# Two transformer blocks on one core: all low parts of the mixers' weights on VectorE, softmax scaling, score copies and conv biases on ScalarE, conv steps at 1.3 per tile

## The chip, the core and the metric

The kernel runs on one core of a Trainium2 chip. The metric is the device time in microseconds (us) of one execution. The kernel before takes 2652.18 us, the median of three runs (2651.34 to 2655.23). One more execution was profiled; it took 2647.99 us, and its span, from the first to the last recorded instruction, is 2646.2 us.

## What is computed

The input is a sequence of 256 tokens of width 1024 in fp32, with a second sequence of 256 tokens, the context. A first block of two layers (called layer 0 and layer 1 here) runs over both sequences, then a second block of two layers runs over the first sequence alone. Only the first block's mixer matters for the change:

```python
proj = h @ p['w_in']                      # h: layernorm, scaled and shifted; 9760 columns
k, v, kg, vg, gf, gb = _mem_parts(...)    # attention keys/values; GLA keys/values, two log gates
q, qg, r, glu, gates = _rest_parts(...)
o_att = softmax(q k^T / sqrt(128)) v      # 8 heads of 128, 2 key/value heads
lg = log_sigmoid(glr @ w_a2 + b_a) / 16   # log gates, cumulated over the tokens
o_gla = gated linear attention, forwards and backwards, with exp(b_i - b_j) between tokens
y = a * sigmoid(g)                        # conv: depthwise, 31 taps, plus bias, layernorm, silu
out = (g_att * (o_att @ w_att_o) + g_gla * (o_gla' @ w_gla_o) + g_conv * (y' @ w_conv_o)) @ w_out
```

Layer 0 does this for both sequences, 512 tokens. Layer 1 does it for the first sequence, 256 tokens, and takes from the context only keys, values and gates. A feed-forward part of 2816 columns follows each mixer.

## The kernel before

**Products in two parts.** Every large product of fp32 operands is made of three TensorE products. An operand is split in a high part (a cast, `whi` for weights) and a low part (the operand minus its high part, `wlo`), and `mm_fm` (lines 386 to 388) and `mm_tm` (467 to 469) add high by high, high by low and low by high. The weights come from HBM as `raw` tiles of 1 MB; `wsplit` (line 357) makes the high part on ScalarE (line 362) and the low part by a subtraction (the helper `tt`, line 288). Which engine subtracts is decided by `pool_lo`: with 0 always VectorE, with 1 always GpSimd (the profile's POOL), with 2 every second time GpSimd:

```python
on_pool = self.pool_lo and self.nsplit % self.pool_lo == 0
```

There are three buffers each for high and low parts and two for `raw`. In the mixers `pool_lo` comes from `PLO0` and `PLO1`: the first number holds from the start of the mixer to the end of the attention's merge, the second from there on. `post`, which follows the mixer, sets it to 1 for its own products; the change leaves that as it is.

**A mixer's order of work.** After an opening in layer 0 that loads and normalizes the input, `mixer` projects the conv's two inputs a and g (16 tiles of 128 columns, 512 tokens wide in layer 0 and 256 in layer 1), then attention keys and values, queries, the gates' small input, and GLA keys and queries. Merge 0 projects the attention's output gates, flushes the attention and projects its result with `w_att_o`; merge 2 does the conv's output, merge 1 that of GLA.

**Background lanes.** Beside these projections run generators, called lanes: the conv's taps, the head transposes, attention, the gates, GLA scores and the modulation vectors (ada). After each tile (or each pair of weight rows) `tick` gives each lane its rate of steps, and `flush` runs a lane to its end. A step of `conv` is two taps for each of two channel groups, so four instructions (the helper `stt`, line 291); a pair of groups has 15 steps, and there are four pairs. `CRATE0 = 1.6` is the number of such steps per tile in layer 0, `CRATE1 = 1.0` in layer 1. Before merge 2 the lanes `gla` (gates) and `conv` are flushed, and `conv_norm` follows.

**What orders an engine's queue.** Instructions are traced in the order of this code, each with a priority. A scheduler then fixes one order for each engine from priorities and its own idea of when inputs are ready. Weight splits have a priority ahead of their place (`WP = -100`), taps one far behind (`CP = 600`). On the chip every engine executes its order as it stands, and an instruction that waits holds what is behind it.

**Names in the rows.** `ca` is a conv accumulator, `gt` the gated conv input, `cw` the taps' weights, `P` the softmax numerators, `PT` their transposes, `s` small columns such as maxima and reciprocals, `zm` and `e` the two terms of a log gate, `B` its cumulative sum, `eq` and `ek` the gate factors of GLA queries and keys, `A` GLA scores, `qn` and `ra` normalized and rotated heads, `pm` and `ps` PSUM tiles, `hTh` and `hTl` transposed heads.

Of the kernel before, what the change touches and what calls it, by code (L numbers as in the profile page):

```python
# [24 lines left out]
CRATE0 = 1.6  # L25
# [6 lines left out]
PLO0A = 1  # L32
PLO0B = 0
PLO0 = PLO0A, PLO0B
PLO1A = 2
# [152 lines left out]
class Builder:  # L188
# [383 lines left out]
    def tabs0(self):  # L572
        nc, I = self.nc, self.I
        rw = lambda n: I[n].rearrange("l (j p) -> (l j) p", p=128)
        self.vt0 = self.vectab("vt0", [rw("conv_b_dw"), rw("conv_ln_g"), rw("conv_ln_b"),
                                       I["gla_b_a"].rearrange("l d (j p) -> (l d j) p", p=128), rw("gla_norm")])
        self.vt0h = self.cp.tile([128, 68], F32, name="vt0h")
        self.ts(self.vt0h, self.vt0, 0.5)
        self.masks = self.cp.tile([128, 160], U32, name="masks")
        nc.sync.dma_start(self.masks, I["masks"])  # L580
        self.ptot = self.cp.tile([128, 2, 4], F32, name="ptot")
# [120 lines left out]
    def ln_tile(self, s, t, fast=True):  # L702
# [6 lines left out]
        m = self.small(1)  # L709
        self.ts(m, mv[:, 0:1], -1.0)  # L710
        nmr = self.small(1)
        self.tt(nmr, m, r, ALU.mult, self.nc.gpsimd)
# [207 lines left out]
    def attention(self, units, tm=False):  # L920
# [6 lines left out]
        def norm(i):  # L927
            for j, (P, sm) in enumerate(st[i]):
                r = self.small(1)
                nc.vector.reciprocal(r, sm)  # L930
                if tm:
                    st[i][j] = P, r
                else:
                    self.ts(P, P, r)
# [116 lines left out]
    def gla_logs(self, l, glrT, T, streams):  # L1051
# [13 lines left out]
        for d in range(2):  # L1065
            es, zs = [], []
            for h in range(4):
# [3 lines left out]
                bias = self.vt0[:, col : col + 1]  # L1071
# [4 lines left out]
                self.ts(m, z, bias, 0.0, ALU.add, ALU.min)  # L1076
# [5 lines left out]
            for h in range(4):  # L1082
                g = zs[h]
                self.tt(g, g, es[h], ALU.subtract)
                for si, s in enumerate(streams):
                    gs = g[:, si * 256 : si * 256 + 256]
                    o = B[d, s, h // 2][:, h % 2, :]
                    if d == 0:
                        nc.vector.tensor_tensor_scan(out=o, data0=self.onesk[:, 0:1].to_broadcast([128, 256]), data1=gs, initial=0.0, op0=ALU.mult, op1=ALU.add)
                    else:  # L1090
                        nc.vector.memset(o[:, 0:1], 0.0)
                        nc.vector.tensor_tensor_scan(out=o[:, 1:256], data0=self.onesk[:, 0:1].to_broadcast([128, 255]), data1=gs[:, 0:255], initial=0.0,
                                                     op0=ALU.mult, op1=ALU.add)
                        self.tt(self.ptot[:, s, h : h + 1], o[:, 255:256], gs[:, 255:256], ALU.add)
# [3 lines left out]
    def gla_states(self, kg, vg):  # L1098
# [6 lines left out]
        def A(i):  # L1105
# [3 lines left out]
            if d == 0:  # L1109
                self.tt(e, b[:, :, 255:256].to_broadcast([128, 2, 256]), b, ALU.subtract, nc.gpsimd)  # L1110
                self.act(e, e, AF.Exp, scale=1.0 / 16)
            else:
                self.act(e, b, AF.Exp, scale=1.0 / 16)
# [27 lines left out]
    def gla_scores(self, xs, kg, qg, A):  # L1141
# [5 lines left out]
        def expo(i):  # L1147
# [14 lines left out]
            self.act(eq, eq, AF.Exp, scale=1.0 / 16)  # L1162
            self.tt(ekv[:, :, 0, :], rb, Bv[:, :, 0, :], ALU.subtract, g)
            self.tt(ekv[:, :, 1, :], Xv[:, :, 1, :], rx, ALU.subtract, g)
            self.act(ek, ek, AF.Exp, scale=1.0 / 16)
# [14 lines left out]
        def mm(i):  # L1180
# [6 lines left out]
            if lv >= 32:  # L1187
# [6 lines left out]
                for jt in range(2):  # L1194
# [3 lines left out]
                    else:  # L1198
                        for b in range(2):
                            r = slice(64 * b, 64 * b + 64)  # L1200
                            nc.vector.tensor_copy(At[jt][r, :, it * 128 + 64 * b : it * 128 + 64 * b + 64],
# [15 lines left out]
            if lv == 0:  # L1217
                for t in range(2):
                    for b in range(4):
                        r = slice(32 * b, 32 * b + 32)  # L1220
                        c = t * 128 + 32 * b
                        nc.vector.tensor_copy(At[t][r, :, c : c + 32], a32.rearrange("p (h t) i -> p h t i", t=2)[r, :, t, :])
# [3 lines left out]
    def gla_out(self, l, xs, qg, vg, A, put, done):  # L1226
# [5 lines left out]
        def init(i):  # L1232
# [8 lines left out]
            self.act(e, self.B[0, s, pr].rearrange("p a b -> p (a b)"), AF.Exp, scale=1.0 / 16)  # L1241
# [4 lines left out]
            self.act(e2, e2, AF.Exp, scale=1.0 / 16)  # L1246
# [71 lines left out]
    def conv(self, l, cts, glu, acc, csum, cw, ns):  # L1318

        v = lambda x: x.rearrange("p (s t) -> p s t", s=ns)  # L1320
        with self.pri(CP):
            for c in cts:
                self.ts(acc[c], glu[c], cw[:, c, 15:16], self.vt0[:, 8 * l + c : 8 * l + c + 1], ALU.mult, ALU.add)
# [21 lines left out]
    def conv_norm(self, l, acc, csum, oact, T):  # L1345
# [31 lines left out]
        def scale(j):  # L1377
# [3 lines left out]
            self.ts(z, z, b, None, ALU.add)  # L1381
            ts[j] = self.u((128, T), F32, "ct")
            self.act(ts[j], z, AF.Tanh)
# [799 lines left out]
```

## Time and profile before

| | |
|---|---|
| median of three runs | 2652.18 us |
| profiled execution | 2647.99 us |
| its span | 2646.2 us |
| TensorE busy with matmuls | 2442.5 us, 92% of the span |
| VectorE busy | 1710.3 us, 65% |
| ScalarE busy | 1118.7 us, 42% |
| GpSimd busy | 786.7 us, 30% |
| HBM | 341.85 MB read, 130 GB/s over the span |
| mean granted clock of TensorE | 0.97 |

The shares are means over stages with different limits: the mixer of layer 0 lies at 66 to 486 us and its GLA part up to about 680, layer 0's rest up to about 1310, the mixer of layer 1 at 1310 to 1640 with its GLA part up to 1780, and the rest belongs to layer 1's feed-forward part and the second block. In the rows PE is TensorE, PEld its weight loads, DVE VectorE, ACT ScalarE, POOL GpSimd. L288 is the line of the kernel that issued the instruction; since a helper issues all subtractions, the tile names tell them apart. A matmul's recorded duration overlaps that of the next one, so the distance of two starts is its cost.

### The profile page before, as it was taken

The numbers are of one execution on the slowest core, as the hardware profiler recorded it, in microseconds if no ns is written. First come the engines' busy times: TensorE is split into PE (matmuls) and PEld (weight loads), VectorE is DVE, ScalarE is ACT, GpSimd is POOL, SyncE is SP. The second block draws the span as 40 slices with busy tenths as digits, with TensorE's granted clock in tenths as the row PEclk, the third lists the DMA queues.
The fourth block names the chain that finished last, engine by engine and source line by source line (L and its number), as shares of the span: only waits on it lengthen the run. The fifth ranks groups of instructions, "written<-read, shape, count | busy, mean of one in ns | idle before, by whom it ended". The sixth has DMA issues, their size and how long they took to land. (4 is left out here: it accounts for less than half of the span.)

```text
span 2646.2 us, 38822 instructions
## 1 busy us (share of the span) xinstructions
PE 2442.5 (92%) x15227; PEld 2089.7 (79%) x15227; DVE 1710.3 (65%) x2803; ACT 1118.7 (42%) x2063; POOL 786.7 (30%) x554
## 2 busy tenths in 40 slices
PE   7768889989999899999987998898999999999998
PEld 5556678777887777876886888887997989888997
DVE  5768997898345733343699879967654556546664
ACT  3113336644343422122343574554453544446443
POOL 2775531577002400101543125714035010112001
PEclk9889899999999999999989999999999999999999
DMA  7323211222334245355243224444574446653454
GB/s 245 128 70 114 64 52 48 80 65 80 112 128 159 85 142 188 113 190 199 83 125 98 67 88 123 132 138 140 175 241 127 128 131 207 202 160 101 148 185 157
DMA packets 277690, 345.41 MB, mean 131 GB/s; under 512 B 12894, under 2 KB 208888, under 8 KB 277508
## 3 DMA queue, kind: packets, MB, share of 16 engines
q1 hardware_dynamic: 277508, 342.94, 40.1%
q8 instruction: 120, 1.97, 0.3%
q14 instruction: 62, 0.51, 0.1%
HBM read 341.85 MB, written 1.05 MB: 130 GB/s over the span
## 5 line engine op out<-in xcount | busy, mean ns | idle before, releaser
L388 PE MATMUL pm<-hi,wlo 128*128 128x256 f32 (+1 forms) x2824 | 912.6, 324 | 31.7 <-POOL wlo L288 17.8
L386 PE MATMUL pm<-hi,whi 128*128 128x256 f32 (+1 forms) x2824 | 921.6, 328 | 11.8 <-ACT whi L362 4.2
L387 PE MATMUL pm<-lo,whi 128*128 128x256 f32 (+1 forms) x2824 | 915.2, 325 | 2.4 <-DVE lo L288 1.4
L362 ACT CAST whi<-raw 128x1024 fp32r<-128x1024 f32 (+1 forms) x464 | 484.7, 1048 | 895.0 <-PE pm L387 518.4
L288 DVE TENSOR_TENSOR wlo<-raw,whi 128x1024 fp32r<-128x1024 f32 (+1 forms) x357 | 452.3, 1270 | 355.7 <-ACT whi L362 355.3
L388 PEld LDWEIGHTS pm<-hi,wlo 128*128 128x128 f32 x2824 | 543.7, 193 | 75.3 <-POOL wlo L288 19.5
L386 PEld LDWEIGHTS pm<-hi,whi 128*128 128x128 f32 x2824 | 542.9, 193 | 55.8 <-ACT whi L362 6.7
L387 PEld LDWEIGHTS pm<-lo,whi 128*128 128x128 f32 x2824 | 544.4, 193 | 50.1 <-issue 7.4
L288 POOL TENSOR_TENSOR wlo<-raw,whi 128x1024 fp32r<-128x1024 f32 (+2 forms) x115 | 353.6, 3085 | 419.8 <-ACT whi L362 386.0
L291 DVE SCALAR_TENSOR_TENSOR ca<-gt,cw,ca 128x482 f32<-128x482 f32 (+29 forms) x480 | 331.6, 746 | 0.0
L468 PE MATMUL pm<-wlo,hi 128*128 128x512 f32 x536 | 216.1, 403 | 25.1 <-POOL wlo L288 25.1
L467 PE MATMUL pm<-whi,hi 128*128 128x512 f32 x536 | 217.3, 405 | 13.2 <-ACT whi L362 6.5
L469 PE MATMUL pm<-whi,lo 128*128 128x512 f32 x536 | 214.2, 400 | 0.0
L288 POOL TENSOR_TENSOR hl<-hr,hh 128x512 fp32r<-128x512 f32 (+1 forms) x38 | 54.8, 1444 | 470.1 <-ACT hh L454 321.4
L288 POOL TENSOR_TENSOR s<-s,mhalf 128x1 f32<-128x1 f32 (+2 forms) x82 | 68.1, 831 | 378.8 <-DVE s L295 375.2
L468 PEld LDWEIGHTS pm<-wlo,hi 128*128 128x128 f32 x536 | 103.9, 194 | 49.7 <-POOL wlo L288 28.2
L467 PEld LDWEIGHTS pm<-whi,hi 128*128 128x128 f32 x536 | 104.1, 194 | 39.8 <-ACT whi L362 7.3
L469 PEld LDWEIGHTS pm<-whi,lo 128*128 128x128 f32 x536 | 103.8, 194 | 22.2 <-DVE lo L291 0.4
L288 POOL TENSOR_TENSOR hl<-raw,hh 128x512 fp32r<-128x512 f32 x24 | 35.9, 1515 | 234.5 <-ACT hh L432 232.2
L288 POOL TENSOR_TENSOR eq<-B 128x256 f32<-128x256 f32 x96 | 89.7, 953 | 28.8 <-DVE lo L288 15.9
L467 PE MATMUL pm<-hh,hi 128*128 128x512 f32 (+2 forms) x258 | 92.6, 362 | 5.9 <-ACT hh L432 3.3
L288 POOL TENSOR_TENSOR ek<-B 128x256 f32<-128x256 f32 (+1 forms) x100 | 95.6, 975 | 3.9 <-PE ps L1209 2.0
(327 smaller groups left out, 3470.8 us busy)
## 6 DMA issues: line engine op xcount, KB each, us to landing
raw<-in_w_in_dram SPq DMA_DIRECT2D x84, 1024.0 KB
aw<-in_w_ada_dram SPq DMA_DIRECT2D x192, 256.0 KB
raw<-in_w_gate_up_dram SPq DMA_DIRECT2D x40, 1024.0 KB
raw<-in_w_ff_gate_dram SPq DMA_DIRECT2D x21, 1024.0 KB
raw<-in_w_ff_up_dram SPq DMA_DIRECT2D x21, 1024.0 KB
raw<-in_w_down_dram SPq DMA_DIRECT2D x20, 1024.0 KB
raw<-in_w_ff_down_dram SPq DMA_DIRECT2D x18, 1024.0 KB
raw<-in_w_att_o_dram SPq DMA_DIRECT2D x8, 1024.0 KB
```

What stands on the lines that cost most here:

```text
L288: return (eng or self.nc.vector).tensor_tensor(out=out, in0=a, in1=b, op=op)
L291: return self.nc.vector.scalar_tensor_tensor(out=out, in0=a, scalar=s, in1=b, op0=op0, op1=op1)
L362: self.nc.scalar.copy(hi, src)
L386: mm(out, lhsT=hi[:, k, :], rhs=a.hi[k], start=(first and k == 0), stop=False)
L387: mm(out, lhsT=hi[:, k, :], rhs=a.lo[k], start=False, stop=False)
L388: mm(out, lhsT=lo[:, k, :], rhs=a.hi[k], start=False, stop=(last and k == nk - 1))
L467: f(p, lhsT=a.hi[kk][:, sl], rhs=hi, start=first, stop=False)
L468: f(p, lhsT=a.hi[kk][:, sl], rhs=lo, start=False, stop=False)
L469: return f(p, lhsT=a.lo[kk][:, sl], rhs=hi, start=False, stop=last)
```

## The change

`PLO0A` and `PLO1A` become 0: all low parts of weights in the mixers' first half are made by VectorE. 80 subtractions move from GpSimd to VectorE, 49 in layer 0 and 31 in layer 1. From VectorE to ScalarE go the scaling of 48 softmax tiles by their reciprocal sums, 72 copies of GLA scores (48 of 32 partitions, 24 of 64), the 16 first conv instructions with the bias, and the 16 additions of the conv norm's bias; the tanh there takes its bias itself. In the log gates, min(z + b, 0) becomes ScalarE's relu(-z - b) with the sign turned, and the subtraction of the second term goes into the scan, which now adds two arrays; the exponentials that follow get the scale -1/16. The negative mean times the reciprocal deviation in `ln_tile` moves from GpSimd to VectorE in one instruction. `CRATE0` becomes 1.3. The core of the diff:

```diff
-CRATE0 = 1.6
+CRATE0 = 1.3
-PLO0A = 1
+PLO0A = 0
-PLO1A = 2
+PLO1A = 0
@@ tabs0
+        self.vt0n = self.cp.tile([128, 16], F32, name="vt0n")
+        self.ts(self.vt0n, self.vt0[:, 48:64], -1.0)
@@ ln_tile
-        m = self.small(1)
-        self.ts(m, mv[:, 0:1], -1.0)
         nmr = self.small(1)
-        self.tt(nmr, m, r, ALU.mult, self.nc.gpsimd)
+        self.stt(nmr, mv[:, 0:1], -1.0, r, ALU.mult, ALU.mult)
@@ attention, norm
-                    self.ts(P, P, r)
+                    self.act(P, P, AF.Copy, scale=r)
@@ gla_logs
-                self.ts(m, z, bias, 0.0, ALU.add, ALU.min)
+                self.act(m, z, AF.Relu, scale=-1.0, bias=neg)
...
-                g = zs[h]
-                self.tt(g, g, es[h], ALU.subtract)
...
-                        nc.vector.tensor_tensor_scan(out=o, data0=self.onesk[:, 0:1].to_broadcast([128, 256]), data1=gs, initial=0.0, op0=ALU.mult, op1=ALU.add)
+                        nc.vector.tensor_tensor_scan(out=o, data0=gs, data1=es_, initial=0.0, op0=ALU.add, op1=ALU.add)
@@ gla_states, gla_scores, gla_out: each exponential of B
-            self.act(eq, eq, AF.Exp, scale=1.0 / 16)
+            self.act(eq, eq, AF.Exp, scale=-1.0 / 16)
@@ gla_scores, mm
-                            nc.vector.tensor_copy(At[jt][r, :, it * 128 + 64 * b : it * 128 + 64 * b + 64],
+                            nc.scalar.copy(At[jt][r, :, it * 128 + 64 * b : it * 128 + 64 * b + 64],
...
-                        nc.vector.tensor_copy(At[t][r, :, c : c + 32], a32.rearrange("p (h t) i -> p h t i", t=2)[r, :, t, :])
+                        nc.scalar.copy(At[t][r, :, c : c + 32], a32.rearrange("p (h t) i -> p h t i", t=2)[r, :, t, :])
@@ conv
-                self.ts(acc[c], glu[c], cw[:, c, 15:16], self.vt0[:, 8 * l + c : 8 * l + c + 1], ALU.mult, ALU.add)
+                self.act(acc[c], glu[c], AF.Identity, scale=cw[:, c, 15:16], bias=self.vt0[:, 8 * l + c : 8 * l + c + 1])
@@ conv_norm, scale
-            self.ts(z, z, b, None, ALU.add)
             ts[j] = self.u((128, T), F32, "ct")
-            self.act(ts[j], z, AF.Tanh)
+            self.act(ts[j], z, AF.Tanh, bias=b)
+            self.act(z, z, AF.Identity, bias=b)
```

VectorE's queue in the a/g projections of layer 0, in the first pair of conv groups (`ca_127`, `ca_128`), before: taps alone.

```order
L291 SCALAR_TENSOR_TENSOR ca_128<-gt_667,cw_683,ca_128 128x2x244
L291 SCALAR_TENSOR_TENSOR ca_127<-gt_664,cw_683,ca_127 128x2x245
L291 SCALAR_TENSOR_TENSOR ca_128<-gt_667,cw_683,ca_128 128x2x245
L291 SCALAR_TENSOR_TENSOR ca_127<-gt_664,cw_683,ca_127 128x2x246
L291 SCALAR_TENSOR_TENSOR ca_128<-gt_667,cw_683,ca_128 128x2x246
```

The same place of VectorE's queue in the changed kernel:

```order
L291 SCALAR_TENSOR_TENSOR ca_128<-gt_661,cw_677,ca_128 128x2x244
L288 TENSOR_TENSOR wlo_869<-raw_866,whi_868 128x1024
L291 SCALAR_TENSOR_TENSOR ca_127<-gt_658,cw_677,ca_127 128x2x245
L291 SCALAR_TENSOR_TENSOR ca_128<-gt_661,cw_677,ca_128 128x2x245
L291 SCALAR_TENSOR_TENSOR ca_127<-gt_658,cw_677,ca_127 128x2x246
L291 SCALAR_TENSOR_TENSOR ca_128<-gt_661,cw_677,ca_128 128x2x246
L291 SCALAR_TENSOR_TENSOR ca_127<-gt_658,cw_677,ca_127 128x2x247
L291 SCALAR_TENSOR_TENSOR ca_128<-gt_661,cw_677,ca_128 128x2x247
L288 TENSOR_TENSOR wlo_904<-raw_866,whi_903 128x1024
```

The low parts `wlo` of the next weight tiles now stand between the taps, here with six taps between two of them; elsewhere in these projections there are up to eight.

VectorE's queue in the flush of the attention in merge 0 of layer 0, one unit of it, before (`lo` is the low part of an attention output):

```order
L930 RECIPROCAL s_2981<-s_2928 128x1
L295 TENSOR_SCALAR P_2927<-P_2927,s_2981 128x512
L930 RECIPROCAL s_2984<-s_2931 128x1
L295 TENSOR_SCALAR P_2930<-P_2930,s_2984 128x512
L288 TENSOR_TENSOR PT_2939<-ps_2933,PT_2938 128x512
L947 TENSOR_REDUCE s_2989<-ps_2987 128x1
L288 TENSOR_TENSOR lo_2059<-ps_2972,hi_2051 128x256
L947 TENSOR_REDUCE s_2990<-ps_2988 128x1
```

And in the changed kernel:

```order
L947 TENSOR_REDUCE s_3111<-ps_3109 128x1
L291 SCALAR_TENSOR_TENSOR ca_134<-gt_1189,cw_677,ca_134 128x2x255
L288 TENSOR_TENSOR lo_2022<-ps_3094,hi_2014 128x256
L947 TENSOR_REDUCE s_3112<-ps_3110 128x1
L291 SCALAR_TENSOR_TENSOR ca_133<-gt_1152,cw_677,ca_133 128x2x254
L930 RECIPROCAL s_3151<-s_3128 128x1
L291 SCALAR_TENSOR_TENSOR ca_134<-gt_1189,cw_677,ca_134 128x2x254
L288 TENSOR_TENSOR PT_3139<-ps_3133,PT_3138 128x512
L930 RECIPROCAL s_3154<-s_3131 128x1
```

The scalings of `P` are gone, and taps of the last pair of conv groups (`ca_133`, `ca_134`), which before were done ahead of this place, stand between the attention's instructions; 27 of them in this flush of nine units.

ScalarE's queue at the same place, before: exponentials, the copy of the transposed scores, and the high part of an output.

```order
L298 ACTIVATE P_3377,s_3378<-ps_3359,s_3361 128x512
L298 ACTIVATE P_3380,s_3381<-ps_3360,s_3362 128x512
L302 CAST PT_3388<-ps_3383 128x512
L302 CAST hi_2055<-ps_3392 128x256
L298 ACTIVATE P_3425,s_3426<-ps_3407,s_3409 128x512
```

In the changed kernel:

```order
L298 ACTIVATE P_3127,s_3128<-ps_3109,s_3111 128x512
L298 ACTIVATE P_3130,s_3131<-ps_3110,s_3112 128x512
L302 CAST PT_3138<-ps_3133 128x512
L298 ACTIVATE P_3127<-P_3127,s_3151 128x512
L298 ACTIVATE P_3130<-P_3130,s_3154 128x512
L302 CAST hi_2015<-ps_3142 128x256
L298 ACTIVATE P_3175,s_3176<-ps_3157,s_3159 128x512
```

The two scalings of a unit stand behind its exponentials and ahead of the next unit's, and each reads a reciprocal that VectorE makes.

## Rows read from the trace of the kernel before

**Rows 1.** Busy time by stretch: stretch, length, engines (instructions), granted clock, DMA share, GB/s

```profile
66.00:486.00 420.00, 353.45 (x1685) 283.44 (x1686) 330.04 (x512) 152.72 (x325) 207.76 (x66) 0.91 0.25 80
402.00:444.00 42.00, 41.98 (x286) 36.98 (x285) 33.18 (x82) 23.35 (x63) 0.65 (x1) 1.00 0.02 4
1310.00:1640.00 330.00, 285.92 (x1870) 260.86 (x1870) 284.84 (x511) 163.69 (x298) 111.52 (x69) 0.94 0.33 102
```

**Rows 2.** TensorE's waits, 66 to 486 us: who, for whom, total us, times, longest

```profile
PE pm L468 <- POOL wlo L288: 22.3, 3, 16.3
PE pm L388 <- POOL wlo L288: 15.3, 2, 12.9
...
PE ps L969 <- DVE P L295: 4.9, 2, 3.3
```

**Rows 3.** GpSimd in order of time: start, duration (us), instruction, idle time before

```profile
118.73 2.39 POOL L288 TENSOR_TENSOR wlo<-raw,whi 128x1024 fp32r<-128x1024 f32 x1 [3.50 <-ACT whi L362]
...
142.61 27.29 POOL L288 TENSOR_TENSOR wlo<-raw,whi 128x1024 fp32r<-128x1024 f32 x1 [2.40 <-ACT whi L362]
```

**Rows 4.** VectorE in order of time, runs of taps, first shape shown

```profile
71.30 16.83 DVE L291 SCALAR_TENSOR_TENSOR ca<-gt,cw,ca 128x482 f32<-128x482 f32 x26
...
1384.96 8.18 DVE L291 SCALAR_TENSOR_TENSOR ca<-gt,cw,ca 128x241 f32<-128x241 f32 x21
```

**Rows 5.** Stretches of 5 us behind TensorE's waits for GpSimd, columns of rows 1

```profile
90.00:95.00 5.00, 4.61 (x13) 3.66 (x14) 5.00 (x8) 0.00 (x0) 5.00 (x2) 0.66 0.00 0
...
110.00:115.00 5.00, 4.37 (x11) 3.46 (x12) 0.00 (x0) 0.00 (x0) 5.00 (x3) 0.54 0.68 198
...
170.00:175.00 5.00, 5.00 (x12) 3.94 (x13) 0.00 (x0) 0.00 (x0) 4.55 (x2) 0.50 0.32 77
...
195.00:200.00 5.00, 3.42 (x8) 2.75 (x9) 0.00 (x0) 0.37 (x1) 5.00 (x3) 0.66 0.46 135
```

**Rows 6.** TensorE in order of time, two matmuls of 512 columns

```profile
78.27 0.39 PE L388 MATMUL pm<-hi,wlo 128*128 128x512 f32 x1
78.50 0.39 PE L386 MATMUL pm<-hi,whi 128*128 128x512 f32 x1
```

**Rows 7.** VectorE by line, 66 to 486 us: count, busy us, mean ns, idle before

```profile
L291 DVE SCALAR_TENSOR_TENSOR ca<-gt,cw,ca 128x482 f32<-128x482 f32 (+14 forms) x240 | 193.5, 861 | 0.0
L295 DVE TENSOR_SCALAR P<-P,s 128x256 f32<-128x256 f32 (+1 forms) x32 | 17.7, 554 | 0.6
...
L295 DVE TENSOR_SCALAR ca<-gt,cw,vt 128x512 f32<-128x512 f32 x8 | 8.8, 1136 | 0.0
...
L288 DVE TENSOR_TENSOR zm<-zm,e 128x512 f32<-128x512 f32 x8 | 7.5, 942 | 7.7 <-ACT e L298 7.6
...
L295 DVE TENSOR_SCALAR zm<-ps,vt 128x512 f32<-128x512 f32 x8 | 5.8, 741 | 3.9 <-ACT e L298 3.9
```

**Rows 8.** VectorE by line, 1310 to 1640 us

```profile
L291 DVE SCALAR_TENSOR_TENSOR ca<-gt,cw,ca 128x241 f32<-128x241 f32 (+14 forms) x240 | 138.1, 631 | 0.0
L288 DVE TENSOR_TENSOR wlo<-raw,whi 128x1024 fp32r<-128x1024 f32 x35 | 42.8, 1222 | 11.3 <-ACT whi L362 11.3
...
L295 DVE TENSOR_SCALAR P<-P,s 128x512 f32<-128x512 f32 x16 | 9.8, 615 | 0.3
...
L295 DVE TENSOR_SCALAR zm<-ps,vt 128x512 f32<-128x512 f32 x8 | 6.0, 745 | 4.0 <-ACT e L298 4.0
L288 DVE TENSOR_TENSOR zm<-zm,e 128x512 f32<-128x512 f32 x8 | 5.5, 684 | 12.5 <-ACT e L298 12.5
```

**Rows 9.** TensorE's waits, 1310 to 1640 us, columns of rows 2

```profile
PE pm L388 <- DVE wlo L288: 11.9, 4, 4.9
PE ps L915 <- DVE ra L288: 8.4, 6, 2.3
```

**Rows 10.** VectorE by line, whole span: copies of scores

```profile
L1222 DVE COPY A<-A 32x64 f32<-32x64 f32 x48 | 18.3, 382 | 0.7
```

**Rows 11.** ScalarE by line and shape, whole span: an operation from SBUF to SBUF

```profile
L298 ACT ACTIVATE e<-e 128x512 f32<-128x512 f32 x32 | 20.2, 635 | 0.3
```

More of the change, by code (lines that the diff above doesn't have):

```diff
@@ L1070, in gla_logs @@
                 col = 48 + 8 * l + 4 * d + h
-                bias = self.vt0[:, col : col + 1]
+                bias, neg = self.vt0[:, col : col + 1], self.vt0n[:, col - 48 : col - 47]
                 e = self.u((128, T), F32, "e")
@@ L1082, in gla_logs @@
             for h in range(4):
-                g = zs[h]
-                self.tt(g, g, es[h], ALU.subtract)
                 for si, s in enumerate(streams):
-                    gs = g[:, si * 256 : si * 256 + 256]
+                    gs, es_ = (x[h][:, si * 256 : si * 256 + 256] for x in (zs, es))
                     o = B[d, s, h // 2][:, h % 2, :]
                     if d == 0:
-                        nc.vector.tensor_tensor_scan(out=o, data0=self.onesk[:, 0:1].to_broadcast([128, 256]), data1=gs, initial=0.0, op0=ALU.mult, op1=ALU.add)
+                        nc.vector.tensor_tensor_scan(out=o, data0=gs, data1=es_, initial=0.0, op0=ALU.add, op1=ALU.add)
                     else:
                         nc.vector.memset(o[:, 0:1], 0.0)
-                        nc.vector.tensor_tensor_scan(out=o[:, 1:256], data0=self.onesk[:, 0:1].to_broadcast([128, 255]), data1=gs[:, 0:255], initial=0.0,
-                                                     op0=ALU.mult, op1=ALU.add)
-                        self.tt(self.ptot[:, s, h : h + 1], o[:, 255:256], gs[:, 255:256], ALU.add)
+                        nc.vector.tensor_tensor_scan(out=o[:, 1:256], data0=gs[:, 0:255], data1=es_[:, 0:255], initial=0.0, op0=ALU.add, op1=ALU.add)
+                        self.stt(self.ptot[:, s, h : h + 1], gs[:, 255:256], o[:, 255:256], es_[:, 255:256], ALU.add, ALU.add)
             yield
@@ L1110, in A @@
                 self.tt(e, b[:, :, 255:256].to_broadcast([128, 2, 256]), b, ALU.subtract, nc.gpsimd)
-                self.act(e, e, AF.Exp, scale=1.0 / 16)
+                self.act(e, e, AF.Exp, scale=-1.0 / 16)
             else:
-                self.act(e, b, AF.Exp, scale=1.0 / 16)
+                self.act(e, b, AF.Exp, scale=-1.0 / 16)
             self.tt(e, e, kg[0, pr], ALU.mult)
@@ L1161, in expo @@
             self.tt(eqv[:, :, 0, :], rx, Xv[:, :, 0, :], ALU.subtract, g)
-            self.act(eq, eq, AF.Exp, scale=1.0 / 16)
+            self.act(eq, eq, AF.Exp, scale=-1.0 / 16)
             self.tt(ekv[:, :, 0, :], rb, Bv[:, :, 0, :], ALU.subtract, g)
             self.tt(ekv[:, :, 1, :], Xv[:, :, 1, :], rx, ALU.subtract, g)
-            self.act(ek, ek, AF.Exp, scale=1.0 / 16)
+            self.act(ek, ek, AF.Exp, scale=-1.0 / 16)
             e[i] = eq, ek
@@ L1240, in init @@
             e = self.u((128, 512), F32, "qf")
-            self.act(e, self.B[0, s, pr].rearrange("p a b -> p (a b)"), AF.Exp, scale=1.0 / 16)
+            self.act(e, self.B[0, s, pr].rearrange("p a b -> p (a b)"), AF.Exp, scale=-1.0 / 16)
             e2 = self.u((128, 2, 256), F32, "qb")
@@ L1245, in init @@
             e2 = e2.rearrange("p a b -> p (a b)")
-            self.act(e2, e2, AF.Exp, scale=1.0 / 16)
+            self.act(e2, e2, AF.Exp, scale=-1.0 / 16)
             self.tt(e, e, Qf, ALU.mult)
```

## The prediction

> **What bounds the kernel now.** I read the busy time by stretch first. Two thirds of the span (the feed-forward parts and the second block) keep TensorE busy and are not touched. What the change touches are the two mixers, one of layer 0 (66 to 486 us) and one of layer 1 (1310 to 1640 us). There TensorE is busy for 353.5 of 420 us and for 285.9 of 330 us, at a mean granted clock of 0.91 and 0.94, so 66.5 and 44.1 us are idle; VectorE has 330.0 and 284.8 us of work [rows 1].
>
> Then I asked what ended TensorE's waits in layer 0's stretch. 22.3 + 15.3 = 37.6 us are waits for a low part made by GpSimd, and most of that is two waits, of 16.3 and 12.9 us [rows 2]. The reader is to see that these are not a shortage of GpSimd time. A low of 128x1024 takes GpSimd 2.39 us when VectorE is idle, and 27.29 us while VectorE runs convolution taps one behind another [rows 3]. VectorE issues 26 taps in 16.83 us, so 0.647 us each, without a gap [rows 4]; each reads two operands in SBUF, as the low does. GpSimd is shut out until that run ends, and TensorE, in order, stands before the matmul that wants this low.
>
> In the Trainium skill, "SBUF — State Buffer", section "Who interferes with whom", VectorE and GpSimd share one port pair; who comes first has it for a whole instruction, and the other is blocked. The trace agrees that it is a block, but not on its length: 27.29 us is far more than the 0.65 us of one tap [rows 3, 4]. By the rule alone a low would take about 3 us (an estimate: one low and one tap), these two waits would not exist, and moving lows would return nothing; that is the second rival below.
>
> **The change, part by part.** Sums are made against the profiled execution, 2647.99 us, 4.2 us under the median of 2652.18.
>
> *Lows of layer 0 (49 of the 80 that move).* The 37.6 us of waits go. With them goes matmul time at the lower clock: behind each wait the granted clock is 0.66, 0.54, 0.50 and 0.66 in 5 us slices with 4.61, 4.37, 5.00 and 3.42 us of matmuls [rows 5]. A slice loses its busy time times what its clock lacks to 1: 1.6 + 2.0 + 2.5 + 1.2 = 7.3 us, of which I count 6. Together -43.6 us.
>
> *What VectorE takes on in layer 0.* 49 lows of 1.22 us (the row of layer 1 [rows 8]) are 60 us. It gives up 32 softmax scalings (17.7 us), 8 conv biases (8.8), 8 minima and 8 subtractions of the gates (5.8 and 7.5): 39.8 us [rows 7]. And the taps lose their contention: 240 take 193.5 us [rows 7], at 0.647 us they would take 155, so 38 us come back. Net 60 - 39.8 - 38 = -18: VectorE's 330 become 312 us, beside a TensorE stage of 420 - 43.6 = 376. So VectorE fits, and what is late next is the place of a low in its queue. In the a/g projections a low now stands behind 6 to 8 taps (4 to 5 us). A tile of 24 matmuls, one each 0.23 us [rows 6], takes TensorE 5.5 us; 7 taps, a low and half a gate product take VectorE 4.5 + 1.2 + 0.3 = 6.0. Over 9 such tiles this is 5 us behind.
>
> Behind the taps that move later stands the attention stretch (402 to 444 us), where TensorE is full and VectorE has 33.2 us of work [rows 1]. The order puts 27 taps (17.5 us) into nine units of attention and takes out 18 scalings, 10 wide and 8 narrow, at most 10 us at 0.554 us [rows 7]. VectorE then has 41 of 42 us, with nothing to spare: I add 5 us. Together +10 us; the ends are 0 (all hidden) and 37.6 (a low behind taps waits as long as it waited for GpSimd).
>
> *Scaling on ScalarE.* 18 scalings at 0.635 us, the row of ScalarE's nearest SBUF operation of 128x512 [rows 11], are at most 11.4 us in that stretch; ScalarE has 23.4 of 42 us there [rows 1] and holds 35. It costs nothing while ScalarE is under 42. New is that ScalarE waits for VectorE's reciprocal, with the next unit's exponentials and the copies of the transposed scores queued behind it. TensorE waits 4.9 us for the scaling today [rows 2]; that wait may grow as it may go, so zero, and 1 us in each of layer 0's 16 units at worst.
>
> In the Trainium skill, "Perfetto Trace Analysis", section "Optimizing Scalar/DVE Operations", an operation that has a fast mode on VectorE should stay there unless VectorE is saturated. The rows agree on the durations (0.554 us on VectorE, 0.635 on ScalarE [rows 7, 11]); by the rule the move would cost 18 x 0.08 = 1.5 us here instead of nothing, and the sum below would be -45.1 instead of -46.6.
>
> *Layer 1 (31 lows).* Here every second low is VectorE's already, and VectorE is the tighter engine: 284.8 of 330 us [rows 1], and TensorE waits 11.9 us for its lows and 8.4 us for the rotated heads [rows 9]. Lows add 31 x 1.22 = 38 us; scalings, minima and subtractions take 9.8 + 6.0 + 5.5 = 21 us away [rows 8], 8 conv biases some 4. The 240 taps take 138.1 us [rows 8] and would take 94 at the 0.39 us of an undisturbed run (21 in 8.18 us [rows 4]): 44 us come back. Net -31 us of VectorE's work. How much of it reaches TensorE is open: at best both waits, -20 us; at worst, if the contention stays, VectorE is 13 us heavier on the path, +13. I take -8, two fifths of the two waits and nearer to the gain, since the 44 us that come back are worked out from rows of this stretch and the heavier queue is not.
>
> *Score copies.* 48 copies of 32 partitions took VectorE 18.3 us [rows 10]; they stood ahead of the next pair's products. On ScalarE they lie in a stretch with room. Ends -18 and +9 (half of it comes back in ScalarE's queue); I take -5, a good quarter, as VectorE is not always what TensorE waits for there.
>
> *The rest at nothing.* The scans read two arrays instead of an array and a repeated one, in the same number; were the second array paid like a tap's elements (0.647 us for 482, so 1.34 ns each [rows 4]), 32 scans of 256 would cost VectorE 11 us, half of it in each layer, and the same less is the other end. I take nothing, as they run beside the products with `w_att_o`, which fill TensorE. The bias with tanh, the negative mean on VectorE and the table loads lie beside full TensorE stretches; uncovered, some 0.5 us each. The pace of 1.3 moves taps later; its cost is in the +10.
>
> Sum: -43.6 + 10 + 0 - 8 - 5 = -46.6, so 2601.4 for a profiled execution and, 4.2 us higher, about **2606 us** as a median.
>
> **Rivals.**
> *VectorE is freed more than I count.* No wait for its lows in layer 0, both waits in layer 1 gone (-20), score copies -8: -43.6 + 0 - 20 - 8 = -71.6, so 2580. For it speaks that 82 us of contention vanish from the taps; against it that an in-order queue turns little of its idle time into gain.
>
> *The wait changes its name.* The low is late behind taps instead of behind the port: 0.77 us for each of 49 lows is 37.6 us again, and the lower clock comes with it. Then -43.6 + 43.6 = 0 and 2652, within 0.2%. The skill's page above ("SBUF — State Buffer") leads there too. Against it: in the new order no low has more than 8 taps before it, while the old one waited for 26 and more.
>
> *Slower: the taps become the end of layer 0's mixer.* They are traced at 1.3 a tile, run into the merge, and the convolution's norm cannot start before the last one. If taps keep their 0.81 us (193.5 by 240), because ScalarE or DMAs and not GpSimd stretched them, VectorE has 330 + 60 - 39.8 = 350 us; with 50 us in which it must wait for heads, scores and gates (today's 90 us of idle time less the 38 of TensorE's stops) it ends at 400, 24 us behind TensorE's 376. Add 16 us for the longer chain of scaling, 13 in layer 1 and 9 for score copies: -43.6 + 24 + 16 + 13 + 9 = +18, so 2670. It decides from about 390 us of VectorE's work and forced waits on. Against it: the 0.647 us were measured in the same stretch with ScalarE and DMAs at work.
>
> **How the numbers follow.** Forecast 0.64, its own range 2588 to 2626; freed more 0.16; the name changes 0.08; slower 0.12. What a measurement can tell from no change is 0.2%, 5.3 us. Faster: 0.64 + 0.16 + 0.01 = 0.81; same 0.07 and slower 0.12 come from the last two. The range of 8 in 10 takes in most of the first two and stops short of no change: 2574 to 2640.
>
> **What would show it.** Right: no GpSimd low in the mixers, no wait of over 5 us before a matmul in 75 to 200 us, taps at 0.65 us (layer 1: 0.39), TensorE idle under 35 us in layer 0's mixer, feed-forward parts unchanged in length. Wrong: waits for VectorE's lows of some 30 us in layer 0; waits for the scaling in the attention stretch; TensorE standing before the convolution's norm; taps still at 0.8 us.

## The result, and the profile after

The changed kernel takes 2551.51 us (median of 4 runs, 2550.07 to 2553.78) against 2653.70 us in the same rounds: ratio 0.9611, 95% interval [0.9589, 0.9633]. That is 102 us less, where 47 were forecast, and outside the range of 2574 to 2640. One of the four runs of experiment 3 below took 3568.7 us at a granted clock of 0.61 where the others had 0.98, and it is left out of that kernel's median and ratio. Between the two profiled executions the spans differ by 94.3 us (2646.2 and 2551.9), and this is what the parts below add up to.

I cut each mixer at the same instructions in both traces: where the tap weights are transposed, where the first score is made, and where the first square of the convolution's norm is summed. The three rows are layer 0 up to the first score, layer 0 from there to that square, and layer 1 from the tap weights to the last square (columns as in [rows 1]). Before:

```profile
66.20:307.30 241.10, 186.45 (x795) 141.28 (x796) 183.03 (x270) 55.02 (x141) 152.17 (x42) 0.87 0.29 94
307.30:507.50 200.20, 187.02 (x979) 157.46 (x977) 168.11 (x283) 109.16 (x201) 62.30 (x31) 0.98 0.21 65
1330.50:1636.90 306.40, 267.36 (x1732) 243.46 (x1731) 270.53 (x491) 153.67 (x282) 97.53 (x56) 0.95 0.33 100
```

After:

```profile
66.40:252.80 186.40, 172.72 (x795) 134.83 (x795) 154.23 (x247) 59.29 (x149) 19.48 (x15) 0.95 0.38 122
252.80:439.20 186.40, 183.49 (x979) 156.49 (x977) 170.28 (x297) 123.61 (x236) 14.87 (x11) 0.99 0.23 69
1259.70:1545.50 285.80, 264.09 (x1761) 243.46 (x1761) 238.10 (x480) 175.33 (x321) 31.22 (x30) 0.96 0.37 114
```

The parts get shorter by 54.7, 13.8 and 20.6 us. The reader is to split each into TensorE's idle time (length less PE) and its busy time. In the first row idle time falls from 54.7 to 13.7 and busy time from 186.5 to 172.7, for the same 795 matmuls: the granted clock rose from 0.87 to 0.95. In the second idle time falls from 13.2 to 2.9 and busy time by 3.5, in the third from 39.0 to 21.7 and by 3.3. What is left of the 94.3 us is 6.2 in layer 0's linear attention, 3.3 in layer 1's, less 3.7 between the layers and 0.6 ahead of and behind all these parts.

TensorE's waits of the first part after the change, all rows, against [rows 2]:

```profile
PE pm L468 <- DVE wlo L288: 7.1, 1, 7.1
PE ps L915 <- DVE ra L288: 3.2, 1, 3.2
PE pm L467 <- DVE qn L288: 2.2, 1, 2.2
PE ps L915 <- DVE qn L288: 1.2, 2, 0.7
```

No wait for GpSimd is left. What the prediction had not taken into its sum are the other waits of the same part before:

```profile
PE ps L915 <- DVE ra L288: 5.9, 2, 5.6
PE pm L467 <- DVE qn L288: 3.1, 4, 1.3
PE pm L467 <- ACT junk L298: 2.9, 1, 2.9
PE pm L386 <- DVE qn L288: 2.7, 1, 2.7
PE ps L1313 <- DMA cwr<-in_conv_w_dw_dram: 1.7, 2, 1.2
```

With two small ones they are 17.5 us, and 6.6 remain. VectorE by line, layer 0's mixer (66 to 420 us) and then layer 1's (1240 to 1545 us), against [rows 7, 8]:

```profile
L291 DVE SCALAR_TENSOR_TENSOR ca<-gt,cw,ca 128x482 f32<-128x482 f32 (+14 forms) x240 | 164.6, 735 | 0.1
L288 DVE TENSOR_TENSOR wlo<-raw,whi 128x1024 fp32r<-128x1024 f32 (+1 forms) x47 | 58.6, 1249 | 18.1 <-ACT whi L362 17.9
...
L291 DVE SCALAR_TENSOR_TENSOR ca<-gt,cw,ca 128x244 f32<-128x244 f32 (+14 forms) x240 | 103.0, 479 | 0.1
L288 DVE TENSOR_TENSOR wlo<-raw,whi 128x1024 fp32r<-128x1024 f32 x66 | 80.6, 1224 | 36.0 <-ACT whi L362 35.9
```

The taps took 164.6 and 103.0 us, 155 and 94 were forecast; a low 1.25 and 1.22 us, as forecast. VectorE's load came out near the forecast, since other terms offset the taps' 10 us: 306.4 us in the first of these stretches, where 312 were forecast for the mixer, and 251.2 in the second, where 284.8 - 31 = 254 were. What TensorE makes of it was not right.

### The profile page after: what moved, and what is told of

Same layout as the page of the kernel before. It is cut to its first block, busy times and chain, and to the rows that moved or that the text cites. A ratio compares the mean times of both kernels' runs of the same rounds, so it can differ in the third digit from the quotient of the medians.

```text
span 2551.9 us, 38718 instructions
## 1 busy us (share of the span) xinstructions
PE 2418.1 (95%) x15227; PEld 2079.3 (81%) x15227; DVE 1624.0 (64%) x2700; ACT 1180.8 (46%) x2225; POOL 518.1 (20%) x460
## 5 line engine op out<-in xcount | busy, mean ns | idle before, releaser
L288 DVE TENSOR_TENSOR wlo<-raw,whi 128x1024 fp32r<-128x1024 f32 (+2 forms) x437 | 551.6, 1265 | 410.6 <-ACT whi L362 409.2
L291 DVE SCALAR_TENSOR_TENSOR ca<-gt,cw,ca 128x242 f32<-128x242 f32 (+28 forms) x480 | 267.6, 607 | 0.2
L288 POOL TENSOR_TENSOR wlo<-raw,whi 128x1024 fp32r<-128x1024 f32 (+1 forms) x35 | 80.6, 2316 | 95.2 <-ACT whi L362 89.8
L468 PE MATMUL pm<-hl,hi 128*128 128x512 f32 (+2 forms) x258 | 93.0, 362 | 1.3 <-POOL hl L288 1.0
```

Source lines behind the costliest of these rows:

```text
L288: return (eng or self.nc.vector).tensor_tensor(out=out, in0=a, in1=b, op=op)
L291: return self.nc.vector.scalar_tensor_tensor(out=out, in0=a, scalar=s, in1=b, op0=op0, op1=op1)
L468: f(p, lhsT=a.hi[kk][:, sl], rhs=lo, start=False, stop=False)
```

## How the low parts were held up

Before, the low of [rows 3] that is issued at 142.61 us ends 27.29 us later, at 169.90. VectorE beside it, in order of time (start, duration):

```profile
137.88 2.60 DVE L295 TENSOR_SCALAR ca<-gt,cw,vt 128x512 f32<-128x512 f32 x1
140.41 10.94 DVE L291 SCALAR_TENSOR_TENSOR ca<-gt,cw,ca 128x482 f32<-128x482 f32 x17
151.28 0.67 DVE L291 SCALAR_TENSOR_TENSOR gt<-gt,ga 128x512 f32<-128x512 f32 x1
151.89 3.98 DVE L291 SCALAR_TENSOR_TENSOR ca<-gt,cw,ca 128x498 f32<-128x498 f32 x6
155.79 0.15 DVE L295 TENSOR_SCALAR modT<-ps 128x8 f32<-128x8 f32 x1
155.87 0.72 DVE L291 SCALAR_TENSOR_TENSOR ca<-gt,cw,ca 128x504 f32<-128x504 f32 x1
156.52 0.67 DVE L291 SCALAR_TENSOR_TENSOR gt<-gt,ga 128x512 f32<-128x512 f32 x1
157.12 10.59 DVE L291 SCALAR_TENSOR_TENSOR ca<-gt,cw,ca 128x506 f32<-128x506 f32 x16
```

VectorE's queue runs from 142.61 to 167.71 without an idle gap, and the low ends 2.19 us after that, which is about the 2.39 us that a low takes alone. So it did no work for some 25 us. The tap run of 26 in [rows 4] ends at 88.13, and the low under it (a wait of 12.9 us in [rows 2]) ends 2.21 us later; here VectorE did not stand still, its next operation, `adar`, which also reads two arrays, took 2.84 us beside the low.

Not every low is held up for a whole run. GpSimd, then VectorE, at another place before:

```profile
129.61 2.94 POOL L288 TENSOR_TENSOR wlo<-raw,whi 128x1024 fp32r<-128x1024 f32 x1 [3.05 <-ACT whi L362]
...
129.59 3.48 DVE L291 SCALAR_TENSOR_TENSOR ca<-gt,cw,ca 128x486 f32<-128x486 f32 x2
```

This low got in behind a single tap, in the middle of a run, where the second tap started 0.64 us after the first as anywhere in it; the second of the two taps then took 2.85 us. What decides whether GpSimd gets in between two taps is not shown.

## The experiments

Times are medians in us; ratios are to the kernel before in the same rounds. The last four columns are lengths between the same instructions: layer 0 to the first score, from there to the norm's first square, from there to the state's product of the linear attention, and layer 1's mixer.

| kernel | time | ratio, 95% interval | to score | to square | to state | layer 1 |
|---|---|---|---|---|---|---|
| before | 2653.7 | 1 | 241.1 | 200.2 | 247.3 | 306.4 |
| after | 2551.5 | 0.9611 [0.9589, 0.9633] | 186.4 | 186.4 | 241.1 | 285.8 |
| 1 lows only | 2567.7 | 0.9690 [0.9676, 0.9704] | 184.5 | 201.3 | 246.4 | 288.4 |
| 2 all but the lows | 2644.5 | 0.9964 [0.9945, 0.9983] | 231.7 | 202.2 | 241.1 | 314.6 |
| 3 pace 1.6 | 2546.5 | 0.9607 [0.9591, 0.9623] | 182.1 | 185.0 | 241.4 | 286.6 |
| 4 taps read PSUM | 2555.9 | one run | 183.4 | 187.9 | 246.7 | 285.1 |
| 5 scaling back | 2550.6 | 0.9603 [0.9587, 0.9618] | 185.8 | 185.8 | 241.3 | 287.1 |
| 6 score copies back | 2559.1 | 0.9636 [0.9622, 0.9651] | 186.6 | 186.3 | 248.8 | 286.7 |
| 7 pace 1.6, all lows | 2544.6 | 0.9580 [0.9565, 0.9594] | 182.0 | 185.0 | 241.6 | 286.8 |
| 8 gaps for GpSimd | 2656.8 | 1.0008 [0.9993, 1.0024] | 230.8 | 199.5 | 246.4 | 322.5 |
| 9 sums in PSUM | 2575.6 | 0.9716 [0.9703, 0.9729] | 194.5 | 185.0 | 241.1 | 302.8 |
| 10 same, pace 1.6 | 2589.0 | 0.9764 [0.9751, 0.9778] | 203.6 | 183.9 | 241.1 | 299.2 |
| 11 gates back | 2558.4 | 0.9637 [0.9620, 0.9653] | 186.8 | 192.1 | 241.2 | 281.7 |
| 12 bias back | 2554.3 | 0.9620 [0.9599, 0.9641] | 194.1 | 183.1 | 241.6 | 282.0 |

**1, the lows alone, and 2, all but the lows.** Of the kernel before and of the changed one, with only the switches of the lows set.

```diff
-PLO0A = 1
+PLO0A = 0
...
-PLO1A = 2
+PLO1A = 0
```

(Experiment 1; experiment 2 is the reverse of it in the changed kernel.)

> The kernel before with the two numbers PLO0A and PLO1A at 0 and nothing else changed, so VectorE makes all low parts and keeps all its other work; conv pace 1.6. Theory A (the port: GpSimd's lows were what slowed VectorE, and what held TensorE): nearly the whole gain of 102 us is here, 2560 to 2590, with taps at 0.65 to 0.70 us in layer 0. Theory B (the sum of parts: lows remove the long waits, the rest of the gain is VectorE's relief by ScalarE): 2600 to 2615, since VectorE gets 98 us of lows and gives up nothing.

> The changed kernel with PLO0A at 1 and PLO1A at 2 again, so GpSimd makes the same lows as before; everything else as changed, the pace of 1.3 too. Theory A: 2630 to 2655, the waits for GpSimd's lows of some 37 us stay and taps stay over 0.75 us. Theory B: 2590 to 2615, as the relief by ScalarE counts by itself.

The lows alone return 3.1%, so 82 us, all the rest alone 0.4%, so 10 us, and both together 3.9%. The first score comes as early with the lows alone as after the whole change, and not without them. The rest is worth more on top of the lows (16 us between the medians, 21 by the ratios) than alone, most of it in the stretch from the first score to the square: 201.3 us with the lows alone, 202.2 with all but them, 186.4 with both. In the lows-only kernel TensorE is busy for 188.0 of the 201.3 us, so idle for 13.3, as much as before. There TensorE's longest waits in the lows-only kernel are not for lows, but for the transposed probabilities:

```profile
PE ps L995 <- ACT PT L302: 8.2, 4, 3.8
```

**4, the same lows on GpSimd, without the contention.** From before: a tap's third operand is a bank of zeros in PSUM, so that it reads one array from SBUF. The sums of the convolution are left out by that.

```diff
-        self.ps = P(name="ps", bufs=5, space=PSUM)
+        self.ps = P(name="ps", bufs=4, space=PSUM)
+        self.pz = P(name="pz", bufs=1, space=PSUM)
...
-                    self.stt(a, v(glu[c])[:, :, lo + d : hi + d], cw[:, c, k : k + 1], a, ALU.mult, ALU.add)
+                    self.stt(a, v(glu[c])[:, :, lo + d : hi + d], cw[:, c, k : k + 1], v(self.tapz[:, 0 : 256 * ns])[:, :, lo:hi], ALU.mult, ALU.add)
```

> The kernel before, lows on GpSimd, but each conv tap adds a PSUM tile of zeros instead of the accumulator, so that a tap reads one operand in SBUF and one in PSUM (the conv's result is not the reference's; one PSUM buffer fewer for the rest). If GpSimd is shut out by VectorE's two operands from SBUF: its lows take 2.4 to 3.5 us in the a/g projections of layer 0, none over 5, the waits of 16.3 and 12.9 us are gone, and the time is 2590 to 2620 with VectorE as full as before. If a full VectorE, ScalarE or the DMAs slow GpSimd in another way: lows of 15 to 27 us as before, and 2640 to 2660.

All lows of GpSimd from 66 to 250 us (duration min/median/max in ns, first and last start), and in a second fence the two parts of layer 0 by engine:

```profile
L289 POOL TENSOR_TENSOR wlo<-raw,whi x27: 1854/2402/2579, 68.3 to 244.9; 128x1024 fp32r<-128x1024 f32 x26, 128x768 fp32r<-128x768 f32 x1
```

```profile
66.30:249.70 183.40, 170.95 (x795) 132.17 (x796) 171.36 (x265) 54.82 (x142) 80.03 (x42) 0.98 0.38 124
...
249.70:437.60 187.90, 183.75 (x979) 154.43 (x977) 151.10 (x288) 109.52 (x201) 59.55 (x30) 1.00 0.22 69
```

The longest low takes 2.58 us, not 27.29, and the parts of both mixers are as short as after the change within 3 us, although not one low was moved: 2555.9 against 2551.5 us, and 34 us less than the 2590 expected at best. A tap takes 0.72 us in layer 0, as it does with its sum in experiment 1, so it is not the missing sum that makes taps shorter. Idle time (12.5 and 4.2 us), busy time (171.0 and 183.8) and clock are close to those of the changed kernel. So it was the taps' second operand in SBUF that shut GpSimd out, and with the lows left where they were this alone is worth nearly the whole gain (by one run).

**8, one operation with one operand in SBUF after every four taps.**

```diff
+            if n % 2 == 0:
+                with self.pri(CP):
+                    self.ts(acc[cts[0]][:, 0:1], acc[cts[0]][:, 0:1], 1.0)
```

> The kernel before with one more VectorE operation behind every convolution step of four taps: a scaling of one column by 1.0, with one operand in SBUF. Theory A1 (GpSimd gets the port at the first VectorE operation that reads only one array of SBUF): no low in 66 to 200 us takes over 6 us, the two waits of 16.3 and 12.9 us are gone, the time is 2570 to 2620 us, although VectorE has 60 operations more in each mixer (some 4 us). Theory A2 (the port is given up only when VectorE's queue stands still): lows still up to 15 to 27 us, the time 2650 to 2665 us.

GpSimd and VectorE of this kernel in order of time (start, duration), at three lows:

```profile
134.06 24.92 POOL L288 TENSOR_TENSOR wlo<-raw,whi 128x1024 fp32r<-128x1024 f32 x1
...
151.31 0.13 DVE L295 TENSOR_SCALAR ca<-ca 128x1 f32<-128x1 f32 x1
151.37 2.70 DVE L291 SCALAR_TENSOR_TENSOR ca<-gt,cw,ca 128x506 f32<-128x506 f32 x4
154.00 0.13 DVE L295 TENSOR_SCALAR ca<-ca 128x1 f32<-128x1 f32 x1
154.06 2.71 DVE L291 SCALAR_TENSOR_TENSOR ca<-gt,cw,ca 128x510 f32<-128x510 f32 x4
156.70 0.13 DVE L295 TENSOR_SCALAR ca<-ca 128x1 f32<-128x1 f32 x1
156.81 5.48 DVE L291 SCALAR_TENSOR_TENSOR ca<-gt,cw,ca 128x508 f32<-128x508 f32 x2
...
99.44 5.66 POOL L288 TENSOR_TENSOR wlo<-raw,whi 128x1024 fp32r<-128x1024 f32 x1 [3.04 <-ACT whi L362]
...
102.76 0.13 DVE L295 TENSOR_SCALAR ca<-ca 128x1 f32<-128x1 f32 x1
102.86 2.78 DVE L291 SCALAR_TENSOR_TENSOR ca<-gt,cw,ca 128x508 f32<-128x508 f32 x1
...
88.52 2.39 POOL L288 TENSOR_TENSOR wlo<-raw,whi 128x1024 fp32r<-128x1024 f32 x1 [4.99 <-ACT whi L362]
...
88.58 0.14 DVE L295 TENSOR_SCALAR ca<-ca 128x1 f32<-128x1 f32 x1
88.65 2.81 DVE L291 SCALAR_TENSOR_TENSOR ca<-gt,cw,ca 128x502 f32<-128x502 f32 x1
```

The low of 134.06 still takes 24.92 us. Behind seven small operations the next tap starts 0.06 us after them, and GpSimd does not get in; behind the eighth, of 156.70, it starts 0.11 us after, and the two taps that follow take 5.48 us instead of 1.4, beside the end of this low and the next one. The low of 99.44 likewise gets in behind its second small operation, where the distance is again 0.11 us, and not behind its first, where it is 0.06. The longer distance is not GpSimd's doing: it is 0.11 us at 115.78 too, where no GpSimd operation runs. It may come of the next tap reading column 0, which the small operation has just written and which the taps of the first half leave out; that is read from the code and not tested. But the low of 88.52, issued 0.06 us ahead of a small operation, got in at once with only 0.06 us to the next tap, and the low of 129.61 before the change got in with no such operation at all. So a low that already waits was let in at the longer halts here; that VectorE must halt is not shown. Nor is it shown whether the small operation itself leaves GpSimd's port free, or whether a longer one would let GpSimd in.

The gaps did help in one place: from 66 to 320 us two lows take over 5 us where five did before, TensorE's waits for them fall from 37.6 to 23.7 us, and the first score comes 10 us sooner. Layer 1's mixer is 16 us longer (322.5 us), for reasons left open, and the time is the same.

By the Trainium skill, "SBUF — State Buffer", section "Who interferes with whom", an operation of VectorE with at most one SBUF input outside its two-port modes does not contend with GpSimd, and one with two contends with a GpSimd operation that reads SBUF; experiment 4 agrees with that (2.58 us at most). The section calls the shared ports an exclusive lock and, of the two-port modes, says that it is held for one whole instruction; this trace shows 24.9 us through a run of many.

**3, the pace, and 7, the best version.** From after: taps at 1.6 a tile; in 7 also the lows of the adapters behind the feed-forward parts on VectorE.

```diff
-CRATE0 = 1.3
+CRATE0 = 1.6
...
-        pool_lo, self.pool_lo = self.pool_lo, 1
+        pool_lo, self.pool_lo = self.pool_lo, 0
```

> The changed kernel with the pace of the conv steps in layer 0 at 1.6 per tile again. If the pace matters because VectorE's queue would be too full beside lows: 2565 to 2580, with waits of TensorE for VectorE's lows in the a/g projections of 15 us and more. If the pace is of no account: within 5 us of 2551.5.

> The changed kernel with the pace of taps back at 1.6 a tile, which alone gave about 4 us, and the lows of the adapters behind the feed-forward parts on VectorE too. If those lows stand behind VectorE's work as GpSimd's stand behind the port: 2546 to 2549 us, as with the pace alone. If GpSimd is shut out there as well and TensorE waits for it: 2535 to 2545 us. If VectorE's queue there is the tighter one: over 2551.

The slower pace of 1.3 gains nothing: 1.6 is 5 us shorter, with intervals that overlap. With both edits it is 2544.6 us, ratio 0.958, the fastest kernel here and 7 us under the changed one; that the adapters' lows have a part in it is not shown, as the two kernels are 2 us apart and were timed on two chips, and in experiment 3's trace TensorE waits only 2.0 us in all for lows of weights on GpSimd.

**5 and 6, scaling and score copies back on VectorE.**

```diff
-                    self.act(P, P, AF.Copy, scale=r)
+                    self.ts(P, P, r)
```

In 6 both copies, of which the second is:

```diff
-                        nc.scalar.copy(At[t][r, :, c : c + 32], a32.rearrange("p (h t) i -> p h t i", t=2)[r, :, t, :])
+                        nc.vector.tensor_copy(At[t][r, :, c : c + 32], a32.rearrange("p (h t) i -> p h t i", t=2)[r, :, t, :])
```

> The changed kernel with the 64 softmax scalings back on VectorE, nothing else. Theory A (scalings on VectorE are what kept the attention stage of layer 0, from the first transposed head to the convolution's norm, at 185 to 186 us in the two kernels that have them there, against 173.5 us after the change): this stage comes back to 182 to 187 us, and the time is 8 to 13 us over the changed kernel's 2551.5, so 2559 to 2565. Theory B (the prediction's: scaling on ScalarE is worth nothing, the stage is shorter because of the other edits, the gates and the convolution's bias): within 3 us of 2551.5, and the stage stays at 172 to 176 us.

> The changed kernel with both score copies back on VectorE. The prediction counted them at -5 us: then this takes 2555 to 2558 us, and the linear attention of layer 0, from the first transposed gate row to the state's product, is 4 to 7 us longer than the 244.4 us of the changed kernel. Rival (those 8 us came from VectorE having no more contention from GpSimd): within 2 us of 2551.5.

Scaling on ScalarE is worth nothing (2550.6 us): theory A falls, and the prediction's zero holds. (It is 48 scalings that go back, not the 64 of the expectation.) In this kernel VectorE is busy for 176.65 of 185.80 us from score to square, and TensorE is idle for 3.3:

```profile
249.70:435.50 185.80, 182.46 (x979) 154.96 (x977) 176.65 (x329) 106.20 (x204) 14.89 (x11) 1.00 0.22 70
```

The score copies are worth 7.6 us, all in layer 0's linear attention (241.1 back to 248.8 us); 5 were forecast.

**9 and 10, the sums of the taps in PSUM.** From experiment 2, so with the lows on GpSimd: one PSUM bank holds the running sum of one channel tile (and `ps` has four buffers), ScalarE copies it out; 10 at pace 1.6.

```diff
+        for c in cts:
+            pa = self.pz.tile([128, 256 * ns], F32, tag="pz", name=self.nm("pa"))
...
+                    a = v(pa)[:, :, lo:hi]
                     self.stt(a, v(glu[c])[:, :, lo + d : hi + d], cw[:, c, k : k + 1], a, ALU.mult, ALU.add)
+                    if k == 30:
+                        self.act(acc[c], pa, AF.Copy)
```

> All edits of the change but the moved lows (they stand on GpSimd as before), and each convolution accumulator lies in one bank of PSUM instead of in SBUF: taps of one channel tile after another, a copy to SBUF by ScalarE at its end, one general PSUM buffer fewer. A tap then reads one array from SBUF and one from PSUM. Theory A (what held up GpSimd's lows, and through them TensorE, were taps with two operands in SBUF): lows 2.4 to 2.6 us in layer 0's mixer, taps 0.65 to 0.75 us, no wait of TensorE for a GpSimd low above 3 us, and 2535 to 2560 us, against 2644.5 with the same lows and accumulators in SBUF. Theory B (the kernel is helped only when GpSimd's lows are gone, whatever the taps read): 2630 to 2650 us. Rival for the amount: taps of one tile in a row, each waiting for the one before, or the missing PSUM buffer, cost TensorE more than they return: over 2560.

> The same with the pace of taps at 1.6 a tile in layer 0. If the pace costs what it did with lows on VectorE (about 4 us): 3 to 5 us under the run with 1.3. If it mattered only because lows stood behind taps in one queue: within 2 us of it.

The mechanism holds a second time, now with the whole convolution: lows of 2.9 us at most in layer 0's mixer, and 2575.6 us where the same kernel with sums in SBUF takes 2644.5. The amount does not: it is over the 2560 of the rival, and at 1.6 a tile it is 13 us more, where both expectations had less or the same. TensorE waits for other things, in experiment 9's first part and in its layer 1:

```profile
PE pm L387 <- DVE qn L289: 6.8, 1, 6.8
PE ps L916 <- DVE ra L289: 4.1, 1, 4.1
...
PE pm L387 <- ACT mt L299: 13.3, 3, 9.4
```

Whether the missing buffer, the order of one tile after another or the copy at its end makes these is open.

**11 and 12, gates and bias back on VectorE.** In 11 minimum and subtraction as before (with the signs that hang on them), in 12 the convolution's bias.

```diff
-                self.act(m, z, AF.Relu, scale=-1.0, bias=neg)
+                self.ts(m, z, bias, 0.0, ALU.add, ALU.min)
...
+                self.tt(g, g, es[h], ALU.subtract)
```

```diff
-                self.act(acc[c], glu[c], AF.Identity, scale=cw[:, c, 15:16], bias=self.vt0[:, 8 * l + c : 8 * l + c + 1])
+                self.ts(acc[c], glu[c], cw[:, c, 15:16], self.vt0[:, 8 * l + c : 8 * l + c + 1], ALU.mult, ALU.add)
```

> The changed kernel with the gates as before: minimum and subtraction on VectorE, running sums over the difference. Of the 14 to 15 us by which layer 0's stage from the first score to the convolution's first square is shorter after the change than with the lows alone moved, neither the scaling nor the score copies nor the pace has any part; what is left are the gates and the convolution's bias. If it is the gates (VectorE's own operations, some 13 us per layer, stand before TensorE's next operand): this stage comes back from 186.4 to 197 to 202 us and the time is 2560 to 2568 us. If not: 185 to 189 us and within 4 us of 2551.5.

> The changed kernel with the convolution's bias back on VectorE (8 operations in each layer). If it is the bias that shortens the stage from the first score to the convolution's first square: 197 to 202 us there, 2560 to 2568 us. If not: 185 to 189 us there and within 4 us of 2551.5.

From score to square the gates are worth 5.7 us (192.1 against 186.4), where 11 to 16 were expected if they were the cause; layer 1's mixer is 4.1 us shorter with them back. The bias does not lengthen this stretch (183.1), but the one before it by 7.7 us. No single edit brings back the 15 us that lie between the lows alone and the whole change, so how they come together there stays open.

## Why the prediction was wrong, step by step

**What bounds the kernel: right.** The lows were held up by the port, not by a shortage of GpSimd. Experiment 4 shows it without moving a low. How long a block lasts is not settled: 27.29 us through VectorE's whole stream at one place, one tap at another. Both rivals that had the wait come back, under another name or as a late convolution, are out.

**The 37.6 us of waits: right.** They are gone; the one wait for a VectorE low, 7.1 us, is a low behind 20 taps in a row (172.23 to 185.43 us):

```profile
172.23 13.20 DVE L291 SCALAR_TENSOR_TENSOR ca<-gt,cw,ca 128x498 f32<-128x498 f32 x20
185.34 0.67 DVE L288 TENSOR_TENSOR adar<-adar,ab 4x512 f32<-4x512 f32 x1
185.95 1.38 DVE L291 SCALAR_TENSOR_TENSOR ca<-gt,cw,ca 128x504 f32<-128x504 f32 x2
187.25 2.34 DVE L288 TENSOR_TENSOR wlo<-raw,whi 128x1024 fp32r<-128x1024 f32 x2
```

The claim that no low has more than 8 taps ahead of it failed: 29 taps stand between this low and the one before it, and 29 again ahead of the low at 380.84 us, for which TensorE does not wait.

**The step that failed: the queue of VectorE, "+10", with the other waits at nothing.** Layer 0's mixer was forecast 33.6 us shorter (-43.6 + 10) and is 68.5 shorter (54.7 + 13.8). The miss of 35 us has three pieces, from the rows above:
- *Other waits, 21 us.* I took only the waits that name GpSimd. Those for rotated heads, normed heads, sums of squares and tap weights (17.5 us to the first score) fell by 10.9, and the idle time from score to square by 10.3. VectorE makes most of these operands and ran its taps slower. Experiment 4 shows that the waits fall when only the contention goes: idle time 12.5 us in the first part, 4.2 in the second. In the first part the lows alone do it too (14.9 us idle). In the second they do not (13.3), although no GpSimd low is left there either: where VectorE makes the lows itself, the 10.3 us need something of the other edits, and what is open. The contention was priced at the engine that was shut out; the 38 us that came back to the other one were counted as room on VectorE, and none of them as a wait of TensorE.
- *The clock, 11 us.* Busy time fell by 13.7 + 3.5 us, 6 were counted, from four slices of 5 us [rows 5]. The granted clock of the whole first part was 0.87 and is 0.95, of the second 0.98 and 0.99.
- *The queue, 3 us.* Of the 5 us in the a/g projections nothing came, of the 5 in the attention stretch nothing either, but 7.1 in the place above. "Nothing to spare" was wrong: with VectorE busy for 95% (experiment 5) TensorE stood idle for 3.3 of 186 us. The taps that fill VectorE there are wanted only at the end, which would explain it; no run tests that.

**Layer 1, "-8": the size was off.** It measured -20.6 in the mixer, the "at best" end of that step's bounds (-20), and 3.3 more behind it. Most of it are the lows (288.4 us with the lows alone).

**Score copies -5, scaling 0: right**, -7.6 and 0 by experiments 6 and 5. The prediction's 0.554 us on VectorE is a mean over two widths; before, a scaling of 512 columns took 0.627 us and one of 256 0.480. On ScalarE the wide ones took 0.74 us, not 0.635, which cost TensorE nothing. By the Trainium skill, "Perfetto Trace Analysis", section "Optimizing Scalar/DVE Operations", an operation with a fast mode on VectorE is faster there, and moving it to ScalarE may make sense where VectorE is saturated. The durations agree (0.48 us for a wide one on VectorE in experiment 5); the kernel's time tells no difference. The other small edits were not nothing in all: experiment 11 is 7 us slower than the changed kernel, and the stretch from score to square has 5.7 of it.

**The range.** "VectorE is freed more than I count" was the right rival, at 2580 and with 0.16. It was itself too small, as it kept the 6 us of clock and left out layer 0's waits that name VectorE.

## What to carry to other kernels

When a trace shows an engine slowed by another one's stream, price both: the wait for the one that is shut out, and every wait for the one whose operations are stretched; and take the clock's loss over the whole stretch, not over the slices behind the longest waits. VectorE at 95% cost TensorE only 3.3 of 186 us here, where much of what fills it is wanted late, and a single run of 20 taps ahead of one wanted low cost 7.1; so look for the longest run of filler in front of one wanted operand instead of adding up loads. The contention can be tested without moving work, by giving the long stream an operand in PSUM.

## What was not expected of the hardware

A GpSimd operation with operands in SBUF got nothing done for 25 us beside a stream of VectorE operations that read two arrays from SBUF (27.29 us instead of 2.39), and seven one-column operations with one operand among them (experiment 8) did not let it in. Twice in that trace a low that already waited got in where VectorE's next tap started 0.11 instead of 0.06 us after such an operation; another low, before the change, got in behind a single tap at no such distance (2.94 us), so the rule behind it stays open. With one of the two operands in PSUM the longest such operation up to 250 us took 2.58 us, and VectorE's own taps in layer 0 0.72 instead of 0.86 us on average.
